# Memory attention in two lanes with longer steps, its scalings on GpSimd, and the sums for w_down in the token tiles

## The chip, the cores and the metric

The kernel runs on one core of a Trainium2 chip. The metric is the device time of one execution in microseconds (us); the time of a kernel is the median of several runs.

Engines in the profile: PE is TensorE (PEld its weight loads), DVE is VectorE, ACT is ScalarE, POOL is GpSimd, SP is SyncE, which here issues every DMA.

## The reference

One layer of a hybrid encoder on 2048 tokens of width 1024, all in fp32, cut to what matters here:

```python
h = rmsnorm(x, g_mix)
z = h @ w_in
qk_m, v_m, o_m, i_pre, f_pre, qkv_na, q_mem, gate_pre = jnp.split(z, split_idx, axis=-1)
...  # mLSTM: short_conv + silu on qk_m, chunks of 64
# neighbourhood attention: q and k normalised per head (8 heads of 32), window 8 x 16
# memory cross-attention into 256 tokens:
q = rmsnorm(q.reshape(bsz, s, MEM_HEADS, MEM_HEAD_DIM), g_mem_q) * (MEM_HEAD_DIM ** -0.5)
sc = jnp.einsum('bshd,bmhd->bhsm', q, k).astype(jnp.float32)
p = jax.nn.softmax(sc, axis=-1).astype(v.dtype)
return jnp.einsum('bhsm,bmhd->bshd', p, v).reshape(bsz, s, MEM_W)
...  # three branches projected, merged by sigmoid(gate_pre), @ w_out, + x
...  # x + relu(rmsnorm(x) @ w_up) ** 2 @ w_down
```

## The kernel before

An fp32 product is computed as three matmuls of fp32r halves (`mm3`, L232 to L234). The order of TensorE is the order in which the program is written. The other engines get their order from a scheduler with priorities; an instruction written at priority + LOW (100) comes later.

**Phase 1** (0 to 965 us) goes through four blocks of 512 tokens (`block_a`). A block makes products group by group, each 24 matmuls (about 5.45 us at the durations of the table below):

- 4 token groups for q and k of the neighbourhood attention (copied out at L504 to tiles `zna`, each appended to the queue `qkq` as a unit `na_qk`),
- 4 channel groups for the convolution (copied out at L654 to `cz`),
- 4 token groups in halves for its values and for the memory queries (`zm` at L527, `zif` at L528; each `zm` is appended to the queue `memq` as a unit `mem_unit`), 4 for the mLSTM's values, in blocks 2 and 3 another 24 gate groups (L599), and 4 for the output gate.

**The side work.** Every six matmuls the program calls `tick`, four times a group. A tick lets each of three streams take a step: `unit_stream` of `qkq`, `unit_stream` of `memq`, and `na_stream`, the neighbourhood attention itself. A unit is a generator, cut by `yield`. A unit_stream has lanes; a lane takes one unit from the queue, and advances it at the ticks (numbered 0 to 3) that are listed for it. So `yield`s and lanes set how many matmuls lie between two links of a unit's chain.

A unit `na_qk` squares `zna` on ACT, sums on DVE (L919), makes r = (sum/n + eps)^-0.5 on GpSimd (L324 and L325), scales `zna` by r on DVE (L922), is transposed on TensorE, and copied out on ACT and DVE into `stq` and `stk`. A `mem_unit` does the same for `zm` (L1155, L324 and L325, L1158), then scores (`psc`), softmax (L1187 to L1194, tile `me`), transposes into `mpT` (L1206), products with the values (L1214).

`na_unit` loads queries (`naq`), keys (`nak`), values (`nav`) and biases (`nab`) of the neighbourhood attention; its stages use `nsb` (scores) and `npt` (transposes).

**The sums for w_down.** The MLP in phase 3 uses sums of the quarters of its weights. `sums_down(q)` loads two 512 KB units of w_down into `dw` (2 buffers), makes four differences on DVE (L579), and stores them to `s_t` (L101). It is called 16 times, at every third of the 48 gate groups, at priority + LOW.

**Phases 2 and 3** (965 us to the end) are the mLSTM, merging, the output projection and the MLP; the change doesn't touch their code.

Of the kernel before, what the change touches and what calls it, by code (L numbers as in the profile page):

```python
# [12 lines left out]
F32 = mybir.dt.float32  # L13
F32R = mybir.dt.float32r
BF16 = mybir.dt.bfloat16
AF = mybir.ActivationFunctionType
ALU = mybir.AluOpType
# [4 lines left out]
D = 1024  # L22
# [15 lines left out]
NB = S // TB  # L38
# [42 lines left out]
class Body:  # L81
# [245 lines left out]

    def small(self, k, tag):
        self.n += 1
        return self.sm_pool(tag).tile([128, k], F32, name=f"sm_{self.n}", tag=f"sm{tag}{k}", bufs=12 if k < 16 else 6)  # L330

    def sm_pool(self, tag):
        return self.p_a if tag == "l" else self.p_c
# [26 lines left out]
    def load_norm(self, src, gbc, gsrc=None, xt=None):  # L360
        if xt is None:
            xt = self.x_tile(src)
        else:
            self.nc.sync.dma_start(xt, src)
        if gsrc:
            self.nc.sync.dma_start(gbc, gsrc)
        self.prep(xt, gbc, xt, self.x_junk())
        return xt


    def phase_1(self):
        nc, a = self.nc, self.a
        p_a = self.p_a

        nc.scalar.activation(p_a.tile([128, 16], F32, name="warm"), self.mhalf, AF.Exp)
        self.xorder = [(0, t) for t in ORDER_0] + [(b, t) for b in range(1, NB) for t in range(4)]
        self.xhs = []
        self.hT = self.p_h.tile([128, 2, 8, TB], F32R, name="hT", tag="hT", bufs=1)
        self.streams = [self.unit_stream(self.qkq, [(1,)]), self.unit_stream(self.memq, [(0, 2)]), self.na_stream()]
        self.mem_setup()  # L380
        self.bif = p_a.tile([16, 1], F32, name="bif")
        nc.sync.dma_start(self.bif, a["b_if"])
        cw = p_a.tile([128, 4, 6], F32, name="cw")
        nc.sync.dma_start(cw, a["conv_wb"])
        self.cw = p_a.tile([128, 4, 6], F32, name="cws")

        nc.vector.tensor_scalar(self.cw[:, 0:2], cw[:, 0:2], 1.0 / 16, None, ALU.mult)
        nc.vector.tensor_scalar(self.cw[:, 2:4], cw[:, 2:4], 0.5, None, ALU.mult)
        self.gmix = p_a.tile([128, 8], F32, name="gmix")
        nc.sync.dma_start(self.gmix, a["gT_mix"])  # L390
        self.halo = p_a.tile([128, 4, 4], F32, name="halo")
        nc.vector.memset(self.halo, 0.0)
        gna = p_a.tile([128, 2], F32, name="gna_raw")
        nc.sync.dma_start(gna, a["g_na"])
        self.gna = p_a.tile([128, 2], F32, name="gna")
        nc.vector.tensor_scalar(self.gna[:, 0:1], gna[:, 0:1], 32 ** -0.5, None, ALU.mult)
        nc.vector.tensor_copy(self.gna[:, 1:2], gna[:, 1:2])
        for b in range(NB):
            self.na_rate = NA_RATE[b]
            self.block_a(b)  # L400
        self.aux_end = self.na_end = True
        self.drain()
# [33 lines left out]
    def rms_x(self, b):  # L436

        nc = self.nc
        ss = self.small(4, "x")
        for t in range(4):  # L440
            r0 = b * TB + t * 128
            xt = self.x_tile(self.a["x"][r0:r0 + 128])
            nc.scalar.activation(self.x_junk(), xt, AF.Square, accum_out=ss[:, t:t + 1])
            yield
        r = self.rstd(ss, D, "x")
        yield

        self.rb = self.gbc[:, b % 2 * TB:(b % 2 + 1) * TB]
        dg = self.t("zna", [128, 512], 3).rearrange("p (t c) -> p t c", t=4)
        nc.vector.tensor_tensor(dg, self.ident.unsqueeze(1).to_broadcast([128, 4, 128]),  # L450
                                r.unsqueeze(2).to_broadcast([128, 4, 128]), ALU.mult)
        for _ in range(4):
            yield
        p = self.ps("tr")
        nc.tensor.matmul(p, self.ones, dg.rearrange("p t c -> p (t c)"), start=True, stop=True)
        nc.scalar.activation(self.rb, p, AF.Copy)

    def x_tile(self, src):
# [1 line left out]
        xt = self.p_x.tile([128, D], F32, name=f"xt_{self.n}", tag="xt", bufs=XT)  # L460
        self.nc.sync.dma_start(xt, src)
        return xt

    def x_junk(self):
        self.n += 1
        return self.p_x.tile([128, D], BF16, name=f"xq_{self.n}", tag="xq", bufs=1)

    def lhs_tok(self, hT, k, t):
        sl = slice(t * 128, (t + 1) * 128)
# [21 lines left out]
    def block_a(self, b):  # L491
# [5 lines left out]
        for i, t in enumerate(ORDER_0 if b == 0 else range(4)):  # L497
            if i == 0 or b == 0 and i < 3:
                self.trans_x()
            if b == 0 and i == MEM_R:  # L500
                self.mem_rms()
            p = self.tok_group(hT, w, t)
            z = self.t("zna", [128, 512], 3)
            nc.scalar.activation(z, p, AF.Copy)  # L504
            self.qkq.append(self.na_qk(b, t, z.rearrange("p (a b) -> p a b", b=32)))
        if b + 1 < NB:
# [23 lines left out]
        for g in {0: [0], 1: [1, 2], 2: [3, 4], 3: [5, 6, 7]}[b]:  # L530
            self.na_ready.append(g)
        self.jobs += [None, None, lambda: self.if_rows(b, zif)]
        w = self.take(4)
        for t in range(4):
            if t == PREP_V and b + 1 < NB and b not in GATES_1:
                self.prep_x()
            p = self.tok_group(hT, w, t)
            s = self.ev()
            nc.scalar.activation(s, p, AF.Copy)
            self.store(self.scr["v"][b][t * 128:(t + 1) * 128], s)  # L540
        if b in GATES_1:
            for j in range(24):
                if j == 22 and b + 1 < NB:
                    self.prep_x()
                self.gate(b, j)
                if j % 3 == 0:
                    self.sums_down(8 * GATES_1.index(b) + j // 3)
        w = self.take(4)
        for t in range(4):
            if t:  # L550
# [17 lines left out]
    def sums_down(self, q):  # L568


        nc = self.nc
        prio = self.tc.cur_priority
        self.tc.cur_priority = prio + LOW
        r = [self.t("dw", [128, 1024], 2) for _ in range(2)]
        for half in range(2):
            nc.sync.dma_start(r[half], self.a["w_units"][self.down[half * FF // 256 + q][0]])
        (b11, b21), (b12, b22) = ((x[:, 0:512], x[:, 512:1024]) for x in r)
        for out, x, y in ((b12, b12, b11), (b22, b22, b12), (b21, b21, b22), (b11, b22, b11)):
            nc.vector.tensor_tensor(out, x, y, ALU.subtract)  # L579
        for half in range(2):  # L580
            self.store(self.scr["t"][q // 2][:, half, :, q % 2], r[half].rearrange("p (n c) -> p n c", n=2))
        self.tc.cur_priority -= LOW
# [330 lines left out]
    def na_qk(self, b, t, z):  # L913
# [5 lines left out]
        nc.vector.tensor_reduce(ss, sq, AX.X, ALU.add)  # L919
        r = self.rstd(ss, 32, "q")  # L920
        yield
        nc.vector.tensor_tensor(z, z, r.unsqueeze(2).to_broadcast([128, 16, 32]), ALU.mult)  # L922
        yield
        pt = self.ps("tr", (128, 4, 128))
        zf = z.rearrange("p a b -> p (a b)")
# [24 lines left out]
    def na_stream(self):  # L950
# [5 lines left out]
        while True:  # L956
# [1 line left out]
                g = self.na_ready.pop(0)  # L958
                todo += [(g, hg, half) for hg in range(2) for half in range(2)]
            if todo and not fetched and (cur is None or cur["h"] > 0):  # L960
                last = self.na_unit(*todo.pop(0), last)
                fetched.append(last)
                biases += [(last, h) for h in range(4)]
            if cur is None and not fetched and self.na_end and not prev and not ready:
# [44 lines left out]
            nc.sync.dma_start(k[ds, :, :nr * 64].bitcast(F32), ks[:, :, lk])  # L1009
        return q, k  # L1010

    def na_unit(self, g, hg, half, before):

        nc = self.nc
        kr0 = min(max(4 * g - 4, 0), 24)
        nr = 8 if g in (0, 7) else 11
        u = dict(g=g, hg=hg, half=half, nk=nr * 40, pts=[], h=0, wait=4)
        u["qk"] = before["qk"] if half else self.na_load_qk(g, hg, kr0, nr)
        u["kts"] = [(3 * i, min(3, nr - 3 * i)) for i in range((nr + 2) // 3)]
        u["ho"] = before["ho"] if half else self.t("nho", [128, 2, 256], 1, F32R)  # L1020
# [15 lines left out]
    def na_scores(self, u, h):  # L1036
# [3 lines left out]
        psc = self.ps("mx")  # L1040
        kl = k[:, h, :nk // 40 * 64].rearrange("p (r c) -> p r c", c=64)[:, :, c0:c0 + 40]
        nc.tensor.matmul(psc[:, :nk], q[:, h, u["half"] * 128:u["half"] * 128 + 128], kl, start=True, stop=True)
        sb = self.t("nsb", [128, 512], 3)
        mx = self.small(1, "n")
        nc.vector.tensor_tensor_reduce(sb[:, :nk], psc[:, :nk], u["bias"][h][:, :nk], -1.0, 3e38, ALU.add, ALU.min, mx)
        sm = self.small(1, "n")
# [82 lines left out]
    def mem_rms(self):  # L1129
        nc, a, p_a = self.nc, self.a, self.p_a  # L1130
        mt = p_a.tile([128, 4 * 704], F32, name="mtok", tag="nak", bufs=2)[:, :2 * D].rearrange("p (t c) -> p t c", t=2)
        nc.sync.dma_start(mt, a["mem"].rearrange("(t p) c -> p t c", p=128))
        ss = self.small(2, "x")
        for t in range(2):
            nc.scalar.activation(self.x_junk(), mt[:, t], AF.Square, accum_out=ss[:, t:t + 1])
        rm = self.rstd(ss, D, "m")
        self.memq += [self.mem_keys(t, z, rm[:, t:t + 1]) for t, z in enumerate(self.memz)]

# [9 lines left out]
    def mem_norm(self, z):  # L1148
# [6 lines left out]
        nc.vector.tensor_reduce(ss, sq, AX.X, ALU.add)  # L1155
        r = self.rstd(ss, 64, "m")
        yield
        nc.vector.tensor_tensor(z4, z4, r.unsqueeze(2).to_broadcast([128, 4, 64]), ALU.mult)  # L1158

    def mem_trans(self, z, dst, g):  # L1160

# [7 lines left out]
    def mem_unit(self, b, t, z):  # L1169
        nc = self.nc  # L1170
        yield from self.mem_norm(z)
        yield
        q = self.t("mq", [128, 2, 2, 128], 1, F32R)
        self.mem_trans(z, q, self.gmqk[:, 0:1])
        yield
        yield

        es = []
# [6 lines left out]
        for j in range(2):  # L1185
            nm = self.small(2, "m")
            nc.vector.tensor_reduce(nm, psc[j], AX.X, ALU.max, negate=True)  # L1187
            sm = self.small(2, "m")
            e = self.t("me", [128, 2, 256], 2)
            for p in range(2):  # L1190
                nc.scalar.activation(e[:, p], psc[j][:, p], AF.Exp, bias=nm[:, p:p + 1], accum_out=sm[:, p:p + 1])
            rs = self.small(2, "m")
# [2 lines left out]
            es.append(e)  # L1195
        yield
        yield
        yield
        ptp = []
        for e in es:  # L1200
            tp = self.ps("tr", (128, 4, 128))
            for p in range(2):
                for kt in range(2):
                    nc.tensor.transpose(tp[:, 2 * p + kt], e[:, p, kt * 128:(kt + 1) * 128], self.ident)
            pT = self.t("mpT", [128, 4, 128], 2)
            nc.scalar.activation(pT, tp, AF.Copy)  # L1206
            ptp.append(pT)
            yield
# [367 lines left out]
```

## Time and profile before

| what | value |
|---|---|
| median of 3 runs | 2985.45 us (2985.35 to 2986.06) |
| profiled execution | 2988.64 us |
| its span in the trace | 2986.9 us |
| mean granted TensorE clock | 0.995 |
| PE busy | 2910.6 us, 97% |
| DVE, ACT, POOL busy | 2070.4 us (69%), 1195.1 us (40%), 237.1 us (8%) |

The span runs from the first to the last instruction; 1.74 us of the profiled execution lie outside it. It took 3.19 us more than the median. A row with "[2.50 <-ACT cz L654]" says that the engine was idle for 2.50 us before this instruction, and that the instruction of ACT on line 654 ended the wait.

### The profile page before, as it was taken

The numbers are of one execution on the slowest core, as the hardware profiler recorded it, in microseconds if no ns is written. First come the engines' busy times: TensorE is split into PE (matmuls) and PEld (weight loads), VectorE is DVE, ScalarE is ACT, GpSimd is POOL, SyncE is SP. The second block draws the span as 40 slices with busy tenths as digits, with TensorE's granted clock in tenths as the row PEclk, the third lists the DMA queues.
The fourth block names the chain that finished last, engine by engine and source line by source line (L and its number), as shares of the span: only waits on it lengthen the run. The fifth ranks groups of instructions, "written<-read, shape, count | busy, mean of one in ns | idle before, by whom it ended". The sixth has DMA issues, their size and how long they took to land.

```text
span 2986.9 us, 41900 instructions
## 1 busy us (share of the span) xinstructions
PE 2910.6 (97%) x15028; PEld 2374.8 (80%) x15028; DVE 2070.4 (69%) x3557; ACT 1195.1 (40%) x2198; POOL 237.1 (8%) x389
## 2 busy tenths in 40 slices
PE   8999999999999899999999999999999999999999
PEld 6778788878877677778888888888878888888887
DVE  6676775567654765674769888666676888885666
ACT  6454654344543333342233333543312433344331
POOL 3020210011000322330000000000000000000000
PEclk9999999999999999999999999999999999999999
DMA  8776777867799667789535444766874444466655
GB/s 276 225 253 202 231 227 240 266 217 217 240 283 307 195 199 234 240 276 315 183 110 169 155 152 155 275 191 224 268 235 128 137 155 151 154 226 225 195 182 165
DMA packets 341712, 632.97 MB, mean 212 GB/s; under 512 B 29344, under 2 KB 151008, under 8 KB 341504
## 3 DMA queue, kind: packets, MB, share of 16 engines
q1 hardware_dynamic: 341504, 630.30, 65.4%
q8 instruction: 118, 1.93, 0.3%
q14 instruction: 90, 0.74, 0.1%
HBM read 453.63 MB, written 176.55 MB: 211 GB/s over the span
## 4 chain that ended last, share of the span: by engine, by line
PE 55%; DVE 2%; DMA 2%; issue 1%; ACT 0%; POOL 0%; SPq 0%; DVEq 0%; ACTq 0%; POOLq 0%
PE mm L232 18%; PE mm L234 18%; PE mm L233 18%; PE mm L1339 0%; DVE h L900 0%; DMA og<-s_o 0%; DMA wr<-in_w_units_dram 0%; DMA hf<-s_hf 0%; DVE ev L1495 0%; ACT hf L896 0%; POOL rs L325 0%; DVE acc L1488 0%; DVE ws L177 0%; DVE h L888 0%; DMA X<-s_a 0%
## 5 line engine op out<-in xcount | busy, mean ns | idle before, releaser
L232 PE MATMUL mm<-X,ws 128*128 128x512 f32 x1152 | 448.5, 389 | 0.0
L234 PE MATMUL mm<-X,ws 128*128 128x512 f32 x1152 | 448.2, 389 | 0.0
L233 PE MATMUL mm<-X,ws 128*128 128x512 f32 x1152 | 448.1, 389 | 0.0
L232 PE MATMUL mm<-hT,ws 128*128 128x512 f32 x896 | 375.6, 419 | 12.1 <-ACT cz L654 5.5
L177 DVE TENSOR_TENSOR ws<-wr,ws 128x1024 fp32r<-128x1024 f32 (+1 forms) x212 | 263.0, 1246 | 142.8 <-ACT ws L176 137.7
L234 PE MATMUL mm<-hT,ws 128*128 128x512 f32 x896 | 353.6, 395 | 0.0
L233 PE MATMUL mm<-hT,ws 128*128 128x512 f32 x896 | 353.4, 394 | 0.0
L233 PE MATMUL mm<-X 128*128 128x512 f32 x896 | 348.8, 389 | 2.5 <-DVE X L1462 2.5
L234 PE MATMUL mm<-X 128*128 128x512 f32 x896 | 348.7, 389 | 0.5 <-DVE X L1462 0.5
L232 PE MATMUL mm<-X 128*128 128x512 f32 x896 | 348.7, 389 | 0.4 <-ACT X L1461 0.4
L1461 ACT ACTIVATE X<-X 128x1024 fp32r<-128x1024 f32 x176 | 187.0, 1063 | 319.4 <-DMA X<-s_t 124.5
L1462 DVE TENSOR_TENSOR X<-X 128x1024 fp32r<-128x1024 f32 x176 | 214.3, 1224 | 132.8 <-ACT X L1461 132.0
L176 ACT ACTIVATE ws<-wr 128x1024 fp32r<-128x1024 f32 (+1 forms) x212 | 223.5, 1059 | 164.7 <-PE mm L234 91.8
L232 PE MATMUL mm<-ws,hT 128*128 128x512 f32 (+2 forms) x704 | 260.9, 371 | 9.3 <-ACT cz L654 5.1
L234 PEld LDWEIGHTS mm<-X,ws 128*128 128x128 f32 x1152 | 216.2, 188 | 45.1
L233 PEld LDWEIGHTS mm<-X,ws 128*128 128x128 f32 x1152 | 216.2, 188 | 44.9
L232 PEld LDWEIGHTS mm<-X,ws 128*128 128x128 f32 x1152 | 216.2, 188 | 44.5
L234 PE MATMUL mm<-ws,hT 128*128 128x512 f32 (+2 forms) x704 | 249.8, 355 | 1.1 <-DVE hT L434 1.1
L233 PE MATMUL mm<-ws,hT 128*128 128x512 f32 (+2 forms) x704 | 249.0, 354 | 0.3 <-DVE ws L177 0.3
L202 ACT ACTIVATE ws<-wr 128x512 fp32r<-128x512 f32 x224 | 135.3, 630 | 219.9 <-PE mm L234 139.3
L232 PEld LDWEIGHTS mm<-hT,ws 128*128 128x128 f32 x896 | 170.2, 190 | 54.1 <-issue 9.8
L234 PEld LDWEIGHTS mm<-hT,ws 128*128 128x128 f32 x896 | 169.6, 189 | 39.0
(266 smaller groups left out, 4855.3 us busy)
## 6 DMA issues: line engine op xcount, KB each, us to landing
wr<-in_w_units_dram SPq DMA_DIRECT2D x308, 512.0 KB
s_s<-u SPq DMA_DIRECT2D x32, 1024.0 KB
X<-s_s SPq DMA_DIRECT2D x64, 512.0 KB
X<-s_t SPq DMA_DIRECT2D x64, 512.0 KB
s_g<-ev SPq DMA_DIRECT2D x96, 256.0 KB
ev<-s_g SPq DMA_DIRECT2D x96, 256.0 KB
s_a<-u SPq DMA_DIRECT2D x96, 256.0 KB
X<-s_a SPq DMA_DIRECT2D x48, 512.0 KB
```

Source lines behind the costliest of these rows:

```text
L176: nc.scalar.activation(w[:, 0], raw, AF.Copy)
L177: nc.vector.tensor_tensor(w[:, 1], raw, w[:, 0].bitcast(F32), ALU.subtract)
L202: nc.scalar.activation(hi, src, AF.Copy)
L232: mm(out, lhs[0], rhs[0], start=first, stop=False)
L233: mm(out, lhs[0], rhs[1], start=False, stop=False)
L234: mm(out, lhs[1], rhs[0], start=False, stop=last)
L1461: nc.scalar.activation(hi, src, AF.Copy)
L1462: nc.vector.tensor_tensor(lo, src, hi.bitcast(F32), ALU.subtract)
```

## The change

- **Lanes and steps.** The lane of `qkq` steps at ticks 1 and 3 of a group (before: 1 alone). `na_qk` has five yields for two: six ticks from its start to the scaling (before four), four from there to its transposes (before four). `memq` gets two lanes, one at tick 0 and one at tick 2 (before: one at both). A `mem_unit` has seven yields for nine, each now four ticks apart instead of two.
- **Scaling on GpSimd.** The scalings of `zna` (L922, 16 of 128x512) and `zm` (L1158, 18 of 128x256) move from DVE to GpSimd, in place as before.
- **Buffers.** `zna` 3 to 4, `mq` 1 to 2, `me` 2 to 4, `mpT` 2 to 4; `small` tiles 12 to 9, `nsb` 512 to 480 columns; the scratch tile of squares (`x_junk`) is gone, squares are written in place or into an `ev` tile.
- **Sums for w_down.** `dw` is gone: the units are loaded into the two `xt` tiles that also hold the x of coming blocks. `sums_down` becomes a generator: the loads at gate j with j % 3 = 0, the differences and stores two gates later. Block 2 makes sums 0 to 6, block 3 sum 15 in its group of values and 7 to 14 at its gates.
- **Neighbourhood attention.** A unit that is fetched while none is live waits eight ticks for its loads, not four.

```diff
-        self.streams = [self.unit_stream(self.qkq, [(1,)]), self.unit_stream(self.memq, [(0, 2)]), self.na_stream()]
+        self.streams = [self.unit_stream(self.qkq, [(1, 3)]), self.unit_stream(self.memq, [(0,), (2,)]), self.na_stream()]
...
+            if b == NB - 1 and t % 2 == 0:
+                sums = sums or self.sums_down(15)
+                sums = next(sums, None) and sums
         if b in GATES_1:
+            sums, qs = None, list(range(7)) if b + 1 < NB else list(range(7, 15))
             for j in range(24):
...
-                if j % 3 == 0:
-                    self.sums_down(8 * GATES_1.index(b) + j // 3)
+                if j < 21 or b + 1 == NB:
+                    if j % 3 != 1:
+                        sums = sums or self.sums_down(qs.pop(0))
+                        sums = next(sums, None) and sums
...
+        r = [self.x_tile(self.a["w_units"][self.down[half * FF // 256 + q][0]]) for half in range(2)]
+        yield True
         prio = self.tc.cur_priority
         self.tc.cur_priority = prio + LOW
-        r = [self.t("dw", [128, 1024], 2) for _ in range(2)]
-        for half in range(2):
-            nc.sync.dma_start(r[half], self.a["w_units"][self.down[half * FF // 256 + q][0]])
...
         r = self.rstd(ss, 32, "q")
         yield
-        nc.vector.tensor_tensor(z, z, r.unsqueeze(2).to_broadcast([128, 16, 32]), ALU.mult)
+        yield
+        yield
+        nc.gpsimd.tensor_tensor(z, z, r.unsqueeze(2).to_broadcast([128, 16, 32]), ALU.mult)
+        yield
         yield
         pt = self.ps("tr", (128, 4, 128))
...
-                last = self.na_unit(*todo.pop(0), last)
+                last = self.na_unit(*todo.pop(0), last, 4 if cur else 8)
...
-        nc.vector.tensor_tensor(z4, z4, r.unsqueeze(2).to_broadcast([128, 4, 64]), ALU.mult)
+        nc.gpsimd.tensor_tensor(z4, z4, r.unsqueeze(2).to_broadcast([128, 4, 64]), ALU.mult)
...
-        q = self.t("mq", [128, 2, 2, 128], 1, F32R)
+        q = self.t("mq", [128, 2, 2, 128], 2, F32R)
         self.mem_trans(z, q, self.gmqk[:, 0:1])
-        yield
         yield
...
-            e = self.t("me", [128, 2, 256], 2)
+            e = self.t("me", [128, 2, 256], 4)
...
         yield
         yield
-        yield
         ptp = []
...
-            pT = self.t("mpT", [128, 4, 128], 2)
+            pT = self.t("mpT", [128, 4, 128], 4)
```

**VectorE in block 1, before**: the scaling of a `zna` (L922) stands in the middle of the queue, behind its sum (L919) and ahead of weights (`ws`) and of other units' copies.

```order
L919 TENSOR_REDUCE sm_2317<-sq_2315 128x16
L1049 RECIPROCAL sm_2082<-sm_2080 128x1
L1050 TENSOR_SCALAR nsb_2077<-nsb_2077,sm_2082 128x320
L922 TENSOR_TENSOR zna_2086<-zna_2086,rs_2319 128x512
L177 TENSOR_TENSOR ws_1834<-wr_1833,ws_1834 128x8x128
L177 TENSOR_TENSOR ws_1839<-wr_1838,ws_1839 128x8x128
```

**GpSimd in block 1, now**: each scaling (L925, that was L922) stands directly behind its own power (L325).

```order
L324 TENSOR_SCALAR rs_1988<-sm_1986 128x16
L325 TENSOR_TENSOR rs_1988<-rs_1988,mhalf 128x16
L925 TENSOR_TENSOR zna_1954<-zna_1954,rs_1988 128x512
L1057 MEMSET nsb_2066 128x40
L324 TENSOR_SCALAR rs_2153<-sm_2151 128x16
L325 TENSOR_TENSOR rs_2153<-rs_2153,mhalf 128x16
L925 TENSOR_TENSOR zna_2014<-zna_2014,rs_2153 128x512
```

No scaling is left in VectorE's queue, so nothing there waits for a power; GpSimd's queue has 34 instructions more.

**SP in block 3's gates, before**, at the loads of the neighbourhood attention's group 7, first half of the heads: the two stores of a sum (`s_t`) stand inside the loads.

```order
L1008 DMA naq_0_9653<-s_qs 32x4x256
L1009 DMA nak_0_9654<-s_ks 32x4x512
L101 DMA s_t_191<-dw_9479 128x2x512
L101 DMA s_t_191<-dw_9480 128x2x512
L1008 DMA naq_0_9653<-s_qs 32x4x256
L1009 DMA nak_0_9654<-s_ks 32x4x512
L1008 DMA naq_0_9653<-s_qs 32x4x256
L1009 DMA nak_0_9654<-s_ks 32x4x512
L1025 DMA nav_0_0_9662<-s_vna 120x2x128
```

**SP now**, at the second half of the heads of the same group (before, its loads stood together behind the stores; those of the first half now do): the stores stand ahead, and the loads of the next sum into the same two tiles inside.

```order
L101 DMA s_t_191<-xt_9713 128x2x512
L101 DMA s_t_191<-xt_9715 128x2x512
L1012 DMA naq_1_10030<-s_qs 32x4x256
L461 DMA xt_9983<-in_w_units_dram 128x1024
L461 DMA xt_9985<-in_w_units_dram 128x1024
L1013 DMA nak_1_10031<-s_ks 32x4x512
L1012 DMA naq_1_10030<-s_qs 32x4x256
L1013 DMA nak_1_10031<-s_ks 32x4x512
L1012 DMA naq_1_10030<-s_qs 32x4x256
L1013 DMA nak_1_10031<-s_ks 32x4x512
L1029 DMA nav_1_0_10039<-s_vna 120x2x128
```

The pair of stores has left the first half's loads; the second half's have got a pair of weight loads. From phase 2 on, all engines' queues are the same as before.

## Rows read from the trace of the kernel before

**Rows 1.** Windows, all of phase 1: busy us (x instructions) by engine, clock, DMA share.

```profile
20.00:965.00 945.00, 912.38 (x5762) 749.82 (x5760) 603.20 (x1368) 470.12 (x995) 106.25 (x209) 0.99 0.78 244
```

**Rows 2.** Groups of PE by line: busy, mean ns, idle before, what ended it.

```profile
L232 PE MATMUL mm<-hT,ws 128*128 128x512 f32 x896 | 375.6, 419 | 12.1 <-ACT cz L654 5.5 <-DMA hT<-s_hT 4.0 <-ACT ev L599 2.5
...
L232 PE MATMUL mm<-ws,hT 128*128 128x512 f32 (+2 forms) x704 | 260.9, 371 | 9.3 <-ACT cz L654 5.1 <-ACT zif L528 4.2
...
L1061 PE MATMUL tr<-ident,nsb 128*120 128x128 f32 x480 | 74.8, 276 | 4.8 <-DVE nsb L1050 4.7
...
L1214 PE MATMUL mx<-mpT,mv 128*64 128x128 f32 x256 | 18.4, 279 | 2.1 <-ACT mpT L1206 2.1
```

**Rows 3.** Waits of DVE: us in total, times, longest.

```profile
DVE zna L922 <- POOL rs L325: 42.4, 15, 3.3
...
DVE zm L1158 <- POOL rs L325: 19.9, 18, 1.4
```

**Rows 4.** Timelines of POOL, DVE, ACT and PE, 200 to 209 us: start, duration.

```profile
200.65 2.90 POOL L325 TENSOR_TENSOR rs<-rs,mhalf 128x16 f32<-128x16 f32 x1
...
203.58 0.69 DVE L922 TENSOR_TENSOR zna<-zna,rs 128x512 f32<-128x512 f32 x1 [3.08 <-POOL rs L325]
...
204.91 0.48 ACT L1191 ACTIVATE me<-mx,sm 128x256 f32<-128x256 f32 x1 [6.15 <-DVE sm L1187]
...
208.25 0.59 ACT L654 ACTIVATE cz<-mm 128x512 f32<-128x512 f32 x1
...
208.90 0.50 PE L232 MATMUL mm<-hT,ws 128*128 128x512 f32 x1 [2.50 <-ACT cz L654]
```

**Rows 5.** Timelines of PE at three other places.

```profile
68.44 0.50 PE L232 MATMUL mm<-hT,ws 128*128 128x512 f32 x1 [1.39 <-ACT cz L654]
...
359.55 0.50 PE L232 MATMUL mm<-hT,ws 128*128 128x512 f32 x1 [1.63 <-ACT cz L654]
...
644.05 0.59 PE L1061 MATMUL tr<-ident,nsb 128*120 128x128 f32 x3 [2.57 <-DVE nsb L1050]
```

**Rows 6.** Windows of 30 us, columns as in the first group.

```profile
60.00:90.00 30.00, 26.25 (x147) 22.17 (x146) 24.39 (x49) 11.08 (x23) 7.30 (x4) 0.94 0.87 270
210.00:240.00 30.00, 27.28 (x191) 23.08 (x190) 26.36 (x67) 14.21 (x33) 0.54 (x4) 0.94 0.75 217
360.00:390.00 30.00, 29.76 (x223) 25.57 (x222) 29.40 (x70) 16.15 (x35) 1.03 (x5) 1.00 0.88 281
630.00:660.00 30.00, 25.34 (x143) 20.22 (x142) 17.79 (x47) 11.61 (x25) 8.87 (x11) 0.94 0.69 208
840.00:870.00 30.00, 24.65 (x186) 19.56 (x185) 17.05 (x42) 11.96 (x25) 0.80 (x6) 0.94 0.91 280
```

**Rows 7.** Timelines of PE and SP, 860 to 870 us.

```profile
869.20 0.60 PE L1042 MATMUL mx<-nak,naq 96*128 96x320 f32 x1 [5.35 <-DMA nav<-s_vna]
...
860.67 0.90 SPq L101 DMA_DIRECT2D s_t<-dw  x2
861.62 0.87 SPq L1008 DMA_DIRECT2D naq<-s_qs  x1
```

**Rows 8.** Waits of SP's queue, 440 to 960 us.

```profile
SPq L101 <- DVE dw L579: 34.0, 15, 8.7
```

**Rows 9.** Chain that ended last: start, duration, what.

```profile
1241.81 3.62 DMA wr<-in_w_units_dram
...
2120.63 7.27 DMA wr<-in_w_units_dram
```

**Rows 10.** Groups of POOL by line and shape: columns as in the second group.

```profile
L325 POOL TENSOR_TENSOR rs<-rs,mhalf 128x16 f32<-128x16 f32 x16 | 46.6, 2915 | 1.3
L806 POOL TENSOR_TENSOR rd<-bd,rp 36x512 fp32r<-36x512 f32 x32 | 44.9, 1406 | 56.4 <-PE mx L809 30.2 <-DVE rp L763 25.6
...
L848 POOL TENSOR_TENSOR qw<-qk,wb 128x256 f32<-128x256 f32 x30 | 26.0, 865 | 121.0 <-PE pn L865 79.1 <-DMA wb<-s_w 17.5 <-DMA qk<-s_qk 12.1
```

**Rows 11.** Timelines of POOL and DVE, 1078 to 1080 us.

```profile
1078.42 0.75 POOL L848 TENSOR_TENSOR qw<-qk,wb 128x256 f32<-128x256 f32 x1 [6.43 <-PE pn L865]
...
1078.60 0.59 DVE L883 TENSOR_TENSOR sm<-sm,r_em 128x4 f32<-128x4 f32 x1 [1.68 <-ACT sm L882]
```

More of the change, by code (lines that the diff above doesn't have):

```diff
@@ L329, in small @@
         self.n += 1
-        return self.sm_pool(tag).tile([128, k], F32, name=f"sm_{self.n}", tag=f"sm{tag}{k}", bufs=12 if k < 16 else 6)
+        return self.sm_pool(tag).tile([128, k], F32, name=f"sm_{self.n}", tag=f"sm{tag}{k}", bufs=9 if k < 16 else 6)
     def sm_pool(self, tag):
@@ L366, in load_norm @@
             self.nc.sync.dma_start(gbc, gsrc)
-        self.prep(xt, gbc, xt, self.x_junk())
+        self.prep(xt, gbc, xt, self.t("ev", [128, D], EV[1], BF16))
         return xt
@@ L442, in rms_x @@
             xt = self.x_tile(self.a["x"][r0:r0 + 128])
-            nc.scalar.activation(self.x_junk(), xt, AF.Square, accum_out=ss[:, t:t + 1])
+            nc.scalar.activation(xt, xt, AF.Square, accum_out=ss[:, t:t + 1])
             yield
@@ L448, in rms_x @@
         self.rb = self.gbc[:, b % 2 * TB:(b % 2 + 1) * TB]
-        dg = self.t("zna", [128, 512], 3).rearrange("p (t c) -> p t c", t=4)
+        dg = self.t("zna", [128, 512], 4).rearrange("p (t c) -> p t c", t=4)
         nc.vector.tensor_tensor(dg, self.ident.unsqueeze(1).to_broadcast([128, 4, 128]),
@@ L462, in x_tile @@
         return xt
-    def x_junk(self):
-        self.n += 1
-        return self.p_x.tile([128, D], BF16, name=f"xq_{self.n}", tag="xq", bufs=1)
     def lhs_tok(self, hT, k, t):
@@ L502, in block_a @@
             p = self.tok_group(hT, w, t)
-            z = self.t("zna", [128, 512], 3)
+            z = self.t("zna", [128, 512], 4)
             nc.scalar.activation(z, p, AF.Copy)
@@ L532, in block_a @@
         self.jobs += [None, None, lambda: self.if_rows(b, zif)]
-        w = self.take(4)
+        w, sums = self.take(4), None
         for t in range(4):
@@ L1010, in na_load_qk, with na_unit @@
         return q, k
-    def na_unit(self, g, hg, half, before):
+    def na_unit(self, g, hg, half, before, wait):
         nc = self.nc
@@ L1016, in na_unit @@
         nr = 8 if g in (0, 7) else 11
-        u = dict(g=g, hg=hg, half=half, nk=nr * 40, pts=[], h=0, wait=4)
+        u = dict(g=g, hg=hg, half=half, nk=nr * 40, pts=[], h=0, wait=wait)
         u["qk"] = before["qk"] if half else self.na_load_qk(g, hg, kr0, nr)
@@ L1042, in na_scores @@
         nc.tensor.matmul(psc[:, :nk], q[:, h, u["half"] * 128:u["half"] * 128 + 128], kl, start=True, stop=True)
-        sb = self.t("nsb", [128, 512], 3)
+        sb = self.t("nsb", [128, 480], 3)
         mx = self.small(1, "n")
@@ L1134, in mem_rms @@
         for t in range(2):
-            nc.scalar.activation(self.x_junk(), mt[:, t], AF.Square, accum_out=ss[:, t:t + 1])
+            nc.scalar.activation(mt[:, t], mt[:, t], AF.Square, accum_out=ss[:, t:t + 1])
         rm = self.rstd(ss, D, "m")
```

## The prediction

> **What bounds the kernel now.** I read the windows by phase first, since only phase 1's queues change. In its 945 us after the start TensorE is busy 912.38 us [rows 1], so 32.6 us is all that can be taken there without removing matmuls, plus what the granted clock loses (0.99 on average). TensorE is the bound; what the change is worth is read from its gaps.
>
> Then the groups of TensorE with what ended their idle time [rows 2]. Three sources stand out. Waits for copies out of the convolution (`cz`, 5.5 + 5.1 = 10.6 us) and for `zif` (4.2): a product group is ready, but the copy that frees its PSUM on ACT is late. Waits for `nsb` of the neighbourhood attention (4.7), and for `mpT` of the memory attention (2.1). ACT copies late because ACT waits for something else: so I went back along the chain.
>
> The timelines around 208.90 us show it [rows 4]. GpSimd's power L325 runs from 200.65 for 2.90 us. DVE waits for it 3.08 us at the head of its queue, at L922, with everything behind it. ACT meanwhile waits 6.15 us for a softmax maximum that stands behind L922 on DVE; its exponentials then run one after the other, `cz` is copied only at 208.25, and TensorE has stood still for 2.50 us. DVE waits like this 15 times for `zna` (42.4 us in all, the longest 3.3) and 18 times for `zm` (19.9 us) [rows 3]: 62.3 us.
>
> TensorE pays for few of them. Beside 208.90 the gaps that end directly such a chain are 68.44 (1.39), 359.55 (1.63) and 644.05 (2.57) [rows 5].
>
> The windows of 30 us add the clock [rows 6]: behind or around these gaps it is 0.94 at 60, 210 and 630 us, that is, an average between the two levels of 1.2 and 2.4 GHz. 6% of 30 us are 1.8 us each, 5.4 us for the three.
>
> **The change part by part.**
>
> *Scaling on GpSimd, off DVE.* It takes the 62.3 us of waits out of DVE's queue, since a power and its scaling now follow each other on GpSimd and nothing else of DVE waits between.
> - The four gaps directly behind these waits: 1.39 + 2.50 + 1.63 + 2.57 = **8.1 us** [rows 4, 5]. I take all.
> - The rest of the same kinds: 10.6 + 4.2 + 4.7 = 19.5, less 8.1 = 11.4 us. These lie in the same stages, where DVE and ACT run behind after the waits, but other work makes them late too (from 360 to 390 us DVE is busy 29.40 of 30 us [rows 6], so there it is simply full). Bounds 0 and 11.4; I have nothing that is nearer to one end, and take half, **5.7 us**.
> - The clock: bounds 0 and 5.4 us. One of the three stretches (630 us) has a second cause, the start of a block; I take two thirds, **3.6 us**.
>
> What GpSimd pays: no multiplication of 128x512 is in the trace; the nearest are one of 36x512 at 1.406 us and one of 128x256 at 0.865 us, mean [rows 10]. Taking 1.41 for the `zna` (16 times) and 0.87 for the `zm` (18 times) I get 22.6 + 15.7 = 38 us on an engine that is busy 106.25 of 945 us [rows 1]. It delays a unit's chain by 0.7 us at most against DVE's 0.69 [rows 4], under four ticks of 1.36 us (a group's 24 matmuls by four ticks) that now lie between scaling and transposes: nothing. If that cover were gone, 16 x 0.7 = 11 us would be at stake. The clearing of `nsb` queues behind a scaling on GpSimd; the next scores come a tick or more later, and it costs nothing.
>
> *Lanes and steps.* Six ticks from start to scaling instead of four, twice the distance between the memory unit's scores, `mpT` and its products. The 2.1 us of waits for `mpT` [rows 2] go: the distance from `mpT` to its products grows from some two ticks to four, 2.7 us more. **2.1 us**, bounds 0 and 2.1. No matmul is added. Two units in flight need two of `mq` and four of `me` and `mpT`, which they get. A queue of memory units is drained at a unit per 14 ticks (18 before). Nothing for `small` and `nsb`: a reused buffer was read long before.
>
> *Waiting eight ticks with the neighbourhood attention.* It applies only when no unit is live, at the start of a block's units. The one wait of its scores for a DMA that is worth naming (869.20, below) is not there: units of the groups ahead are live then. Cost: those units end at most four ticks (5.4 us) later, hidden by gate and value groups behind them (blocks 2 and 3) or by the next block's products; without that cover it would be 5.4 us once, at the end of phase 1.
>
> *Sums for w_down.* The work stays the same: 32 loads, 64 differences, 32 stores. What moves is SP's queue. Before, the stores `s_t` wait on SP for the differences 15 times, 34.0 us, longest 8.7 [rows 8]. One of these waits hurts: at 860.67 two stores go out in the midst of group 7's loads, the loads follow at 861.62 and later, and TensorE stands for 5.35 us until 869.20 [rows 7]; the clock there is 0.94 too (1.8 us) [rows 6]: **7.15 us**. In the new order this pair stands behind those loads. But now the next sum's two loads go into the tiles that the last stores read, one gate behind; SP must hold them until these stores have landed, and what is behind on SP is held too. A landing of such a 512 KB piece takes, by the nearest rows, 3.62 to 7.27 us [rows 9]. At group 7's second half exactly this pair stands between `naq` and `nak`. So I let the stall move rather than vanish: +7.15 - 7.15 = **0**. Bounds: 7.15 us of gain (the new place has slack), and a stall at several of the 15 places (below).
>
> *The rest.* The squares' scratch tile, `zna` with 4 buffers: no wait of before hangs on them, nothing.
>
> Sum: 8.1 + 5.7 + 3.6 + 2.1 = 19.5 us. The profiled execution took 2988.64 us (span 2986.9, and 1.74 us around it): 2969.1 us for it. It lay 3.19 us above the median, so in terms of the median 2985.45 - 19.5 = **2966 us**.
>
> *A row and a rule against it.* In phase 2 DVE's L883, on 4 columns, started 0.18 us after a GpSimd multiplication of 0.75 us and lasted 0.59 us: both end at 1079.2 [rows 11]. So a GpSimd multiplication held a small DVE instruction to its end. By the Trainium skill, "SBUF — State Buffer", section "SBUF: two separate sides", DVE and GpSimd share a pair of ports as an exclusive lock for a whole instruction, which a DVE instruction with two SBUF inputs needs too; the trace agrees with it at this place. The sum without it is 2966, with it the first rival's.
>
> **The rivals.** The measure below is that the change is felt by more or less than my 0.2% (6 us, about what a measurement of this kernel can tell from no change).
>
> *GpSimd holds DVE up.* If each of the 38 us of new multiplications blocks DVE as at 1078.42, DVE loses 38 of the 62.3 us it gains. TensorE's gain from DVE's waits is 8.1 + 5.7 + 3.6 = 17.4 us, or 0.28 us per us of wait; 38 x 0.28 = 10.6 us go back. Gain 8.9 us: **2976.5 us**. For it: rows 11, and that much of DVE's work in phase 1 (`ws`, L177) reads two SBUF operands. Against it: most products of a unit come from PSUM, and not each scaling meets such an instruction.
>
> *DVE is full anyway.* The gaps are then made by the load of a stage, not by the waits; the work behind a wait is only sooner done, and TensorE stops at the next late copy. For it: the 29.40 of 30 us at 360. Against it: in the stretches at 60 and 630 us DVE has 24.39 and 17.79 of 30 [rows 6]. It leaves the `mpT` and one gap, 3 to 4 us: **2982 us**, no change that can be measured.
>
> *SP holds the attention's loads (slower).* The place: a pair of weight loads, held until the stores ahead have landed, with `naq`, `nak`, `nav` of the next unit behind it, which then come too late as at 869.20. A stall like this costs 7.15 us. With the old one gone and k new ones the time is -19.5 - 7.15 + 7.15 k; from k = 4 of the 15 places (+2) on it is no gain, and with k = 5 it is +9.1: **2994.5 us**. For it: the order at group 7. Against it: one gate (5.45 us) lies between stores and loads, about a landing, and in the order only seven of the pairs stand next to such loads.
>
> *All of it goes.* All 19.5 us of gaps, the whole clock loss, `mpT` and the stall: 19.5 + 5.4 + 2.1 + 7.15 = 34.2 us: **2951 us**. For it: the waits of 62.3 us are the largest on DVE in phase 1. Against it: the full stretch at 360.
>
> **How the numbers follow.** My forecast 0.42 (its own range, from the bounds of its terms: gain 8.1 + 0 + 1.8 + 2.1 = 12.0 to 8.1 + 11.4 + 5.4 + 2.1 = 27.0 us, so 2958 to 2973.5); GpSimd holds DVE up 0.16; all goes 0.12; DVE full 0.16; slower by SP 0.14. The lock has 0.16 because the one row agrees, but at a place where no engine waited. Faster by over 0.2%: 0.42 + 0.16 + 0.12 = 0.70; same 0.16; slower 0.14. The range goes from the case in which all goes (2950, a little below) to the case without effect, with as much above (2988); outside stay the stalls on SP (0.14) and the ends of the others.
>
> **What would show it.** Right: in the waits of DVE no `zna` or `zm` behind L325; PE's idle time behind `cz`, `zif` and `nsb` at 9 to 12 us instead of 19.5; the granted clock near 1.00 at 60 and 630 us; the wait for `mpT` gone; scalings on GpSimd of about 1.4 and 0.9 us. GpSimd as the new brake: DVE's L177 or sums much longer while a scaling runs than otherwise, ACT waits for DVE as before. DVE full: the same idle time behind `cz` with other releasers. SP: gaps at L1042 ended by `nak` or `nav`, more than one, with SP waiting for `s_t` before a load of `xt`. What would make the prediction wrong above all is a chain that I have costed at nothing because its unit now has more ticks: if a step that comes later in program order is then late for the next block, gaps open at block starts.

## The result: slower, although phase 1 became faster as forecast

The median is 2992.45 us (2987.75 to 2998.03, nine runs), against 2985.45 us before (2983.02 to 2991.23, nine runs). The ratio is 1.0024, 95% interval 1.0015 to 1.0033: slower by 0.24%. The forecast of 2966 us, its range (2950 to 2988) and its sign were wrong.

The profiled execution took 2998.03 us, span 2996.3 us, 9.4 us more than that of before. First the windows of 30 us of the changed kernel, with the columns of [rows 6]:

```profile
60.00:90.00 30.00, 28.57 (x175) 25.05 (x174) 28.06 (x52) 11.99 (x24) 10.32 (x8) 1.00 0.90 292
210.00:240.00 30.00, 30.00 (x246) 28.29 (x245) 25.27 (x69) 12.23 (x32) 7.58 (x12) 1.00 0.63 183
...
630.00:660.00 30.00, 29.57 (x200) 23.58 (x199) 21.03 (x50) 15.99 (x33) 13.88 (x17) 1.00 0.68 195
...
870.00:900.00 30.00, 22.11 (x137) 17.23 (x136) 14.93 (x39) 11.54 (x26) 0.96 (x6) 0.83 0.88 265
```

The three stretches that were at 0.94 are at 1.00. The groups of TensorE, with the columns of [rows 2], and its first groups, of products with X, which had no row ahead of the prediction:

```profile
L232 PE MATMUL mm<-X,ws 128*128 128x512 f32 x1152 | 455.7, 396 | 0.0
...
L232 PE MATMUL mm<-hT,ws 128*128 128x512 f32 x896 | 375.0, 419 | 8.2 <-DMA hT<-s_hT 4.4 <-ACT ev L600 3.8
...
L232 PE MATMUL mm<-ws,hT 128*128 128x512 f32 (+2 forms) x704 | 259.8, 369 | 2.7 <-ACT zif L524 1.8 <-ACT cz L655 0.5 <-ACT ev L515 0.5
...
L1065 PE MATMUL tr<-ident,nsb 128*120 128x128 f32 x480 | 74.5, 275 | 3.1 <-DVE nsb L1054 3.1
...
L1216 PE MATMUL mx<-mpT,mv 128*64 128x128 f32 x256 | 17.5, 279 | 0.0
```

Behind `cz`, `zif` and `nsb` TensorE waits 0.5 + 1.8 + 3.1 = 5.4 us for 19.5, behind `mpT` not at all. So where is the loss? Phase 2 begins with the first `mx<-qk` matmul. Its row in the timeline of TensorE before:

```profile
1018.31 0.71 PE L827 MATMUL mx<-qk 64*128 64x128 f32 x8
```

and in that of the changed kernel:

```profile
1000.54 0.71 PE L828 MATMUL mx<-qk 64*128 64x128 f32 x8
```

Phase 1 ends 17.8 us earlier. All of it, and 9.4 us more, is lost behind it, in code that the change doesn't touch and whose queues are the same. From there to the first product `mm<-X,ws` of the MLP it is 374.6 us before and 376.8 after; from that to the last matmul 1587.7 and 1612.7 us: 25 us. The loss has no gap. It is the pace. The group `mm<-X,ws` of before, one line of three:

```profile
L232 PE MATMUL mm<-X,ws 128*128 128x512 f32 x1152 | 448.5, 389 | 0.0
```

389 ns against 396. Matmuls overlap, so the step from start to start is what counts. The timeline of TensorE before, at 1650 us:

```profile
1649.63 0.39 PE L234 MATMUL mm<-X,ws 128*128 128x512 f32 x1
...
1651.21 0.39 PE L232 MATMUL mm<-X,ws 128*128 128x512 f32 x1
```

These two are seven matmuls apart (the six between them are left out): 1.58 us, 226 ns a step. The changed kernel there:

```profile
1649.76 0.40 PE L233 MATMUL mm<-X,ws 128*128 128x512 f32 x1
...
1651.16 0.40 PE L233 MATMUL mm<-X,ws 128*128 128x512 f32 x1
```

Six matmuls apart: 1.40 us, 233 ns a step. Over all their starts in the trace that follow each other directly, the mean step of `mm<-X,ws` is 226.71 ns before and 233.33 ns after. 3456 of them by 6.6 ns are 22.8 us, nearly all of the 25. The granted clock is 1.00 in both from 1400 to 2000 us, and the products `mm<-X`, both of whose operands are in X, keep their step of 226.7 ns.

What did change is where X lies. The `small` tiles of the pool under it lost 3 buffers in 6 groups, at 32 bytes a tile 576 bytes. The allocator put X at byte 97536 of a partition before, and puts it at 96960 now. ws stays at byte 1280, and its five buffers lie at multiples of 256. Before, X did too (97536 = 381 x 256); now it is 192 bytes past one. A padding of 192 bytes ahead of X (`PAD`) stayed as it was.

### The profile page after: what moved, and what is told of

Its sections match the earlier page's. It is cut to its first block, busy times and chain, and to the rows that moved or that the text cites. A ratio compares the mean times of both kernels' runs of the same rounds, so it can differ in the third digit from the quotient of the medians.

```text
span 2996.3 us, 41916 instructions
## 1 busy us (share of the span) xinstructions
PE 2929.4 (98%) x15028; PEld 2375.1 (79%) x15028; DVE 2066.5 (69%) x3523; ACT 1195.8 (40%) x2198; POOL 268.8 (9%) x423
## 4 chain that ended last, share of the span: by engine, by line
PE 55%; DVE 2%; DMA 2%; issue 1%; ACT 0%; POOL 0%; SPq 0%; DVEq 0%; ACTq 0%; POOLq 0%
PE mm L232 18%; PE mm L233 18%; PE mm L234 18%; PE mm L1341 0%; DMA wr<-in_w_units_dram 0%; DMA hf<-s_hf 0%; DVE h L901 0%; DMA og<-s_o 0%; DVE ev L1497 0%; DVE acc L1490 0%; ACT hf L897 0%; POOL rs L325 0%; DMA X<-s_a 0%; DVE ws L177 0%; DVE h L889 0%
## 5 line engine op out<-in xcount | busy, mean ns | idle before, releaser
L232 PE MATMUL mm<-X,ws 128*128 128x512 f32 x1152 | 455.7, 396 | 0.0
L234 PE MATMUL mm<-X,ws 128*128 128x512 f32 x1152 | 455.4, 395 | 0.0
L233 PE MATMUL mm<-X,ws 128*128 128x512 f32 x1152 | 455.4, 395 | 0.0
L232 PE MATMUL mm<-hT,ws 128*128 128x512 f32 x896 | 375.0, 419 | 8.2 <-DMA hT<-s_hT 4.4
L234 PE MATMUL mm<-hT,ws 128*128 128x512 f32 x896 | 353.2, 394 | 0.0
L233 PE MATMUL mm<-hT,ws 128*128 128x512 f32 x896 | 353.2, 394 | 0.0
L233 PE MATMUL mm<-X 128*128 128x512 f32 x896 | 349.6, 390 | 3.4 <-DVE X L1464 3.4
L234 PE MATMUL mm<-X 128*128 128x512 f32 x896 | 349.3, 390 | 0.5 <-DVE X L1464 0.5
L232 PE MATMUL mm<-X 128*128 128x512 f32 x896 | 349.3, 390 | 0.0
L232 PE MATMUL mm<-ws,hT 128*128 128x512 f32 (+2 forms) x704 | 259.8, 369 | 2.7 <-ACT zif L524 1.8
L234 PEld LDWEIGHTS mm<-X,ws 128*128 128x128 f32 x1152 | 216.4, 188 | 52.3
L232 PEld LDWEIGHTS mm<-X,ws 128*128 128x128 f32 x1152 | 216.4, 188 | 52.2
L233 PEld LDWEIGHTS mm<-X,ws 128*128 128x128 f32 x1152 | 216.5, 188 | 52.1
L234 PE MATMUL mm<-ws,hT 128*128 128x512 f32 (+2 forms) x704 | 249.6, 355 | 2.0 <-DVE hT L434 2.0
L233 PE MATMUL mm<-ws,hT 128*128 128x512 f32 (+2 forms) x704 | 248.9, 354 | 0.0
L232 PEld LDWEIGHTS mm<-hT,ws 128*128 128x128 f32 x896 | 170.1, 190 | 49.7 <-issue 10.7
L234 PEld LDWEIGHTS mm<-hT,ws 128*128 128x128 f32 x896 | 169.6, 189 | 38.9
```

Of the source, the lines that this page charges most:

```text
L232: mm(out, lhs[0], rhs[0], start=first, stop=False)
L233: mm(out, lhs[0], rhs[1], start=False, stop=False)
L234: mm(out, lhs[1], rhs[0], start=False, stop=last)
```

## The experiments

Theory A: the place of X, relative to ws, sets the step. Rival B: the run, the chip or the transfers do it. The first four kernels tell them apart.

**X back in its old place** (the changed kernel):

```diff
-PAD = 192
+PAD = 768
```

> The changed kernel with 768 instead of 192 bytes of padding ahead of X in phases 2 and 3: X starts at byte 97536 of a partition, as before the change (96960 with it). Theory A (the place of X sets the pace of its products with ws): the 3456 matmuls mm<-X,ws go back from 395 to 389 ns and the time falls by 3456 x 6.6 ns = 23 us against the changed kernel, to about 2970, 15 us below the kernel before. Rival B (the slower matmuls come from the run, the chip or the transfers, not from the place): 395 ns stays, time as the changed kernel, 2988 to 2998.

2968.74 us (2963.24 to 2973.66), ratio to before 0.9940 (0.9924 to 0.9956). Its groups of TensorE:

```profile
L232 PE MATMUL mm<-X,ws 128*128 128x512 f32 x1152 | 448.8, 390 | 0.0
```

Step 226.71 ns. 576 bytes of padding take off 24 us, and the kernel is 0.6% faster than before.

**A multiple of 256, but not the old place**: `PAD = 256`.

> The changed kernel with 256 bytes of padding: X at byte 97024, 64 bytes from the slow place, not the place of before, but again a multiple of 256 like ws and hT. Theory A1 (a boundary of 256 bytes or a smaller one decides): 389 ns, time about 2970. A2 (the place of before in steps of 512 bytes or more decides): 395 ns, time 2988 to 2998. Rival B: 395 ns.

2971.43 us, ratio 0.9952 (0.9938 to 0.9967), 389 to 390 ns, step 226.7 ns. 64 bytes more than in the changed kernel are enough: A1.

**Only the small tiles, in the kernel before:**

```diff
-... tag=f"sm{tag}{k}", bufs=12 if k < 16 else 6)
+... tag=f"sm{tag}{k}", bufs=9 if k < 16 else 6)
```

> The kernel before with 9 instead of 12 small tiles a tag, nothing else: X moves to byte 96960 as in the changed kernel. Theory A: mm<-X,ws go from 389 to 395 ns, phase 1 as before, time 2985 + 23 = 3008. Rival B: 389 ns and 2985.

3010.65 us, ratio 1.0079 (1.0065 to 1.0093), step 233.33 ns; phase 2 begins at 1017.51 us, as before. DVE's waits for GpSimd are those of before too (42.3 and 19.9 us). So three buffers fewer of each of six kinds of tiny tile cost 24 us by themselves.

```profile
L232 PE MATMUL mm<-X,ws 128*128 128x512 f32 x1152 | 456.1, 396 | 0.0
```

**X at the slow byte, and ws moved with it** (changed kernel):

```diff
-            self.pad(self.p_ws, 128)
+            self.pad(self.p_ws, 64)
...
-PAD = 192
+PAD = 256
```

> The changed kernel with ws 64 bytes lower (its padding 64 instead of 128) and X at the slow byte 96960: X and ws now have the same remainder of 256 (192), and neither is a multiple of it. If the places of the two operands relative to each other decide: 389 ns, about 2970. If the place of X alone decides: 395 ns, 2988 to 2998. If every operand has to start at a multiple of 256: 395 ns and mm<-hT,ws in phase 1 slower too.

2965.11 us, ratio 0.9932 (0.9915 to 0.9949), step 226.70 ns, with X at the byte at which it was slow, and neither operand at a multiple of 256. It is the distance between the two operands that counts, not the place of one.

**How the step goes with the distance.** Three more kernels:

- `PAD = 128` (changed kernel): X 128 bytes past a multiple.

> The changed kernel with 128 bytes of padding: X at byte 96896, 128 bytes past a multiple of 256, while ws is at one. If a boundary of 128 bytes is enough: mm<-X,ws take 389 ns, about 2970. If it must be 256: 395 ns or another pace, about 2992.

One run, 2988.89 us, 395 ns, step 232.5 ns. 128 is not enough.

- `PAD = 256` in the kernel before: X 64 bytes past.

> The kernel before with 256 instead of 192 bytes of padding ahead of X: X moves by 64 bytes to 97600, nothing else changes. If its place relative to ws decides: mm<-X,ws go from 389 to about 395 ns, all of 23 us of it in phase 3, time about 3008. If 64 bytes are within the same granule: 389 ns and 2986.

One run, 2993.25 us, step 228.9 ns: slower, but a third of what I expected (phase 3 took 10 us more, not 23). The three matmuls of a product don't pay alike: the steps that start at L232, L233 and L234 are 226.9, 229.1 and 230.7 ns.

- ws alone moved by 64 bytes (changed kernel):

```diff
-            self.pad(self.p_ws, 128)
+            self.pad(self.p_ws, 64)
+            self.pad(self.p_h, 64)
```

> The changed kernel with ws alone 64 bytes lower (hT and X stay where the change put them, bytes 43520 and 96960): X and ws share a remainder of 256 again, hT and ws no longer do. If any matmul pays whose two operands lie apart: mm<-X,ws 389 ns (23 us less), but mm<-hT,ws and mm<-ws,hT some 6 ns more each, 4800 matmuls, up to 31 us more: 2995 to 3000. If only the products with X pay: about 2970.

2973.62 us, ratio 0.9958 (0.9944 to 0.9972). The products of X with ws are back at 226.7 ns. X and every tile behind it lie where the change put them, so no tile that moved along with X made the loss. The price went to another pair as far as these are back to back: `mm<-ws,yT`, in the place of hT in phase 3, from 228.5 to 233.2 ns, in the groups of TensorE from 391 to 395 ns:

```profile
L234 PE MATMUL mm<-ws,yT 128*128 128x512 f32 x64 | 25.3, 395 | 0.0
```

Of the 4800 products of phase 1, which I expected to pay up to 31 us, one kind paid. Those with hT moving over ws have a step of 230.2 ns for 230.0 with the change. Those with ws moving over hT have 186.1 for 183.7 as a mean over their widths, but that mean hides where it lies: the 1344 of 512 columns went from 229.4 to 233.3 ns, some 5 us in all. Those of 256 and 272 columns stayed (121.05 and 121.25, 127.2 and 127.3 ns); their units of weights are 1056 columns wide, so that their operands lie at several remainders in both kernels. Phase 2 begins at 1001.78 us, for 1000.54 with the change.

A matmul has a fixed operand (128 columns, which the weight load takes) and a moving one (here 512). The rows name the moving operand first: L1388 of the changed kernel passes ws as the fixed and X as the moving one. All these kernels together, by the byte of the moving operand less that of the fixed one, remainder of 256:

| remainder | mean step, ns | in |
|---|---|---|
| 0 | 226.7 | `mm<-X,ws` of before, X at 97024 and 97536, both moved, ws alone moved |
| 64 | 228.9 | `mm<-X,ws`, X 64 past |
| 128 | 232.5 | `mm<-X,ws`, X 128 past |
| 192 | 233.3 | `mm<-X,ws` of the changed kernel and of 9 small tiles; `mm<-ws,yT` (233.2) and `mm<-ws,hT` of 512 columns (233.3) with ws alone moved |

The kernel with ws alone moved fits at 192: ws moving over yT and over hT pays 4 to 5 ns. At 64 it doesn't quite: hT moving over ws pays 0.2 ns, X over ws 2.2.

**The parts of the change, with X back in its place.** For these I look at the start of phase 2, since a few us in 2970 are near the noise between runs. It lies at 1018.31 us before, and at 1001.63 with `PAD = 768`. It is read from one execution of each kernel, and it has noise too: the changed kernel, `PAD` of 128, 256 and 768, and X and ws both moved have the same phase 1 and begin phase 2 between 997.89 and 1001.63 us.

Scalings back on DVE:

```diff
-        nc.gpsimd.tensor_tensor(z, z, r.unsqueeze(2).to_broadcast([128, 16, 32]), ALU.mult)
+        nc.vector.tensor_tensor(z, z, r.unsqueeze(2).to_broadcast([128, 16, 32]), ALU.mult)
...
-        nc.gpsimd.tensor_tensor(z4, z4, r.unsqueeze(2).to_broadcast([128, 4, 64]), ALU.mult)
+        nc.vector.tensor_tensor(z4, z4, r.unsqueeze(2).to_broadcast([128, 4, 64]), ALU.mult)
```

> The changed kernel with X back at byte 97536, scalings back on DVE, lanes and steps as changed. If the wait for GpSimd's power at the head of DVE's queue makes the gaps: DVE waits again (40 us or more in all for zna and zm), 10 us or more of gaps behind cz, zif and nsb return, time 2979 to 2985. If the longer steps already cover the power: few waits, time about 2969.

2983.55 us, ratio 0.9991 (0.9982 to 1.0000); phase 2 begins at 1012.98, 11.4 us later. The waits of DVE, as [rows 3]:

```profile
DVE zna L925 <- POOL rs L325: 41.0, 16, 3.1
DVE zm L1162 <- POOL rs L325: 17.4, 15, 1.4
```

They are back, and with them gaps behind `cz` (5.0 us; 0.5 with `PAD = 768`), `zif` (3.7; 2.2) and `nsb` (8.7; 5.0), and a clock of 0.94 from 60 to 90 us and of 0.91 from 630 to 660. More ticks for a unit, which are distances on TensorE, hardly shorten these waits (58.4 us for 62.3).

Lanes and yields of before, scalings on GpSimd:

```diff
-        self.streams = [self.unit_stream(self.qkq, [(1, 3)]), self.unit_stream(self.memq, [(0,), (2,)]), self.na_stream()]
+        self.streams = [self.unit_stream(self.qkq, [(1,)]), self.unit_stream(self.memq, [(0, 2)]), self.na_stream()]
...
-        yield
-        yield
         nc.gpsimd.tensor_tensor(z, z, r.unsqueeze(2).to_broadcast([128, 16, 32]), ALU.mult)
         yield
-        yield
```

(and two yields more in `mem_unit`.)

> The changed kernel with X back at byte 97536, but lanes and yields as before the change; the scalings stay on GpSimd. If the scalings' place alone took away the gaps behind cz, zif and nsb: these stay near 5 us in all, only the 2 us behind mpT return, time about 2971. If the longer steps did it: 15 to 20 us of gaps return, time 2984 or more.

2977.09 us, ratio 0.9964 (0.9951 to 0.9977); phase 2 begins at 1006.70, 5.1 us later. DVE has no scaling in its queue and so none of those waits, `cz` has one gap of 2.15 us left, and no `mpT` wait returns: the lanes alone were not what took that wait away. What returned are waits of the neighbourhood attention's scores (L1043, 16.6 us for the 10.6 with `PAD = 768`): 12.9 behind transfers, for 10.1, and 3.0 behind the memory attention's exponentials, for none. The size lies between the two expectations; why the memory attention's steps move these waits I have not settled.

Sums in one place again:

```diff
-                    if j % 3 != 1:
-                        sums = sums or self.sums_down(qs.pop(0))
-                        sums = next(sums, None) and sums
+                    if j % 3 == 0:
+                        for _ in self.sums_down(qs.pop(0)):
+                            pass
```

> The changed kernel with X back at byte 97536 (padding 768) and, in the gate groups, loads, differences and stores of a sum in one place at every third gate, as before the change, but in the xt tiles. If the stall of 8.5 us before the second half of group 7 comes from the loads that wait for the stores one gate before them: it goes, TensorE gains 8.5 us and the clock's loss around it (about 2), time about 2958. Rival: the stall comes back elsewhere, since the stores now wait on SP for the differences, as before the change: time as with padding 768 alone, 2969, with one gap of 5 to 8 us at L1046.

Phase 2 begins at 994.64 us, 7.0 us earlier than with `PAD = 768`; the time is 2970.07 us, ratio 0.9944 (0.9931 to 0.9956). In the changed kernel SP's timeline shows how the wait came about:

```profile
866.21 0.95 SPq L101 DMA_DIRECT2D s_t<-xt  x2
867.21 1.30 SPq L1012 DMA_DIRECT2D naq<-s_qs  x1
872.23 1.62 SPq L461 DMA_DIRECT2D xt<-in_w_units_dram  x2
874.20 0.33 SPq L1013 DMA_DIRECT2D nak<-s_ks  x1
```

The loads at L461 wait for the stores, by SP's waits from 860 to 890 us:

```profile
SPq L461 <- DMA s_t<-xt: 4.5, 2, 3.6
```

TensorE's timeline shows the end of it:

```profile
884.43 0.61 PE L1046 MATMUL mx<-nak,naq 96*128 96x320 f32 x1 [7.89 <-DMA nav<-s_vna]
```

SP holds the second load of the attention from 868.5 to 874.2. Without the two gates the gap is 5.23 us instead (with `PAD = 768` it was 8.53): smaller, ended by a load of `wr`, and the time shows nothing of the 7 us beyond the noise. That is the expectation's rival: a gap of 5 to 8 us at L1046 and the time of `PAD = 768`.

Ten sums in block 2, five in block 3:

> The changed kernel with X back at byte 97536, the loads, differences and stores of a sum in one place, and ten sums in block 2's gates (every second gate), five in block 3's (every fifth), for seven and eight. If block 3's stalls of neighbourhood attention at L1046 come from the transfers being nearly full there (DMA share above 0.9): the gaps of 2.6 and 5.2 us shrink, phase 2 starts some 5 to 8 us earlier, time 2960 to 2965. If block 2 then has the stalls instead: 2970 as with one place alone.

2970.87 us, ratio 0.9943 (0.9929 to 0.9957). The rival was right: block 3's gaps at 816 and 880 us went, and in block 2 and at the start of block 3 others came (2.14, 2.77 and 6.37 us, the last at L1046, 653.03 us); phase 2 begins at 998.62 us. In block 2 the DMA share rose (from 480 to 600 us it is 0.92; with seven sums there in one place it is 0.77 and 0.81 in the two halves), but around the longest new gap, from 640 to 660 us, it is 0.54. So that full transfers make these gaps is not shown.

## Why the prediction was wrong, by its own steps

**The step that failed** is "I read the windows by phase first, since only phase 1's queues change", and with it "Nothing for `small` and `nsb`". The queues of phase 3 are the same, the instructions are the same, and yet 3456 matmuls run 2.9% slower, since a pool under X shrank by 576 bytes. I costed the smaller pool by its buffers' reuse, never by what it moves. No rival had it; that of the stalls on SP came near in time (2994.5 us) by another way. The place of X is worth 24 us both ways (taken out of the change, and put alone into the kernel before), more than all the rest.

**The rest of the sum was nearly right in total, in part by luck.** Phase 1 gave 17.8 us in the profiled run, forecast 19.5, and with X in place the time is 2968.74 us, forecast 2966. But the terms that hang on the scaling's place were forecast at 8.1 + 5.7 + 3.6 = 17.4 us, and undoing it gives back 11.4; lanes and steps were forecast at 2.1, and undoing them gives back 5.1; and the 5.7 was half of a range for which the prediction had no row.
- Gaps behind `cz`, `zif` and `nsb`: forecast 8.1 + 5.7 = 13.8, measured 19.5 - 5.4 = 14.1 (11.8 with `PAD = 768`, the same phase 1). The scaling's place is the main cause (the waits and 11.4 us come back when it is undone). Of the four direct ones, that at 644 us is still there (2.28 us, at 625.93, at the same place in the order of the products, for `nsb`), now without a wait for a power: DVE works from 620.73 us on without a pause, first on x for the coming block (L416, L434).
- Clock: forecast 3.6, measured 5.4 in the three windows.
- `mpT`: forecast 2.1, measured 2.1, but not by the lanes alone: the wait stays away when they are undone.
- Stall on SP: it did move to group 7's second half, as said; but forecast 7.15 - 7.15 = 0, measured 7.89 us and a clock of 0.83 from 870 to 900 us, where before it was 5.35 us and 0.94 to 0.95. It costs some 4 us more than before.
- Lanes: forecast nothing beyond `mpT`, measured 5.1 us, by waits of the neighbourhood attention's scores.

**The rivals.** GpSimd holding DVE up happens, and is small. The changed kernel's timeline of GpSimd:

```profile
184.97 1.05 POOL L925 TENSOR_TENSOR zna<-zna,rs 128x512 f32<-128x512 f32 x1
```

and of DVE there:

```profile
185.15 3.08 DVE L177 TENSOR_TENSOR ws<-wr,ws 128x1024 fp32r<-128x1024 f32 x2 [0.72 <-ACT ws L176]
```

Two weight splits of 1.25 us, the mean, take 3.08: 0.6 us too much, with 0.87 us of the scaling still to run when they began. The Trainium skill, "SBUF — State Buffer", section "SBUF: two separate sides", has a DVE instruction with two SBUF inputs wait for a whole GpSimd instruction that reads SBUF and started first. This row agrees with it roughly. The powers, which read SBUF too, did not hold the splits up, and there the measurement goes against the page: while that of 181.98 us ran, for 2.91 us, a split that began at 182.40 took 1.22 us, and no split that began inside a power took over 1.30. By the lines' usual times only 12 of the 34 scalings hold a DVE instruction up, 6.4 us in all, of my 38; and a scaling took 1.12 us (`zna`) and 0.74 us (`zm`), my estimates were 1.41 and 0.87. One such hold stands ahead of a gap: in DVE's run of work from 620.73 us the eight L416 take 2.99 us, for 2.19 before, with a scaling on GpSimd at 622.28, so up to 0.8 of the 2.28 us at 625.93 are this rival's. DVE full: no, the gaps went. SP: one stall, not five. The slower result came from none of them.

## What to carry to other kernels

A change of a buffer's size or count moves whatever is allocated behind it. Look at the places of TensorE's two operands in the new program as well as at the queues: here matmuls of 512 columns back to back, whose moving and fixed operand differ in their first bytes by a multiple of 256, ran at 226.7 ns a step, and otherwise at up to 233.3. If a stage whose instructions and order haven't changed has another mean duration in the rows, that is where to look, before any wait.

## What the runs showed of the hardware that I had not expected

- The step of a 128x128 by 128x512 fp32r matmul depends on how far apart its two operands start in a partition: 226.7, 228.9, 232.5 and 233.3 ns at remainders of 0, 64, 128 and 192 of 256 bytes, at a granted clock of 1.00 in all cases. Why it does, the runs don't show.
- In phase 1, where steps are longer at a remainder of 0 too, 192 showed (`mm<-ws,hT` of 512 columns, 229.4 and 233.3 ns), and 64 hardly did (`mm<-hT,ws`, 230.0 and 230.2 ns), where `mm<-X,ws` paid 2.2 ns; why is open.
- A GpSimd multiplication of 128x512 took 1.05 us where nothing held it up, 2.05 ns a column; the power on 128x16 in the same place takes 2.9 us, and the weight splits that began while one ran took 1.22 to 1.30 us, their usual time.
